# Two-layer decoder trunk: the high weight half of the SwiGLU products meets both row halves in one 512-column matmul, the two result halves added when the tile is read

## The chip, the core and the metric

The kernel runs on one core of a Trainium2 chip. The metric is the device time of one execution in microseconds (us). Times of three runs are known for the kernel before, and one further execution was recorded by the hardware profiler; its trace is what the rows below come from. In the rows, PE is TensorE's matmul, PEld TensorE's weight load, DVE VectorE, ACT ScalarE, POOL GpSimd and SP SyncE; L12 is line 12 of the kernel.

## What is computed

Two layers of a decoder trunk work on one sequence of 256 positions with a model width of 1024. Each layer has three sub-layers: a SwiGLU, a token mixer (in layer 0 a gated linear recurrence, in layer 1 differential attention), and a second SwiGLU. So there are six sub-layers, s = 0 to 5, and four of them (0, 2, 3, 5) are SwiGLUs. Cut to what matters here:

```
for l in range(2):
    mod = silu(c) @ ada_w[l] + ada_b[l]           # shift, scale, gate of each sub-layer
    pre(h, j) = rmsnorm(h, norm_g[l, j]) * (1 + scale_j) + shift_j
    x = x + 0.5 * (1 + gate_0) * swiglu(pre(x, 0), ffn_wi[l, 0], ffn_wo[l, 0])
    x = x +       (1 + gate_1) * mixer_l(pre(x, 1))
    x = x + 0.5 * (1 + gate_2) * swiglu(pre(x, 2), ffn_wi[l, 1], ffn_wo[l, 1])

swiglu(h, wi, wo):  gt, up = split(h @ wi);  return (silu(gt) * up) @ wo     # 1024 -> 2 x 2816 -> 1024
```

All data are 32-bit floats.

## The kernel before

**Layout.** The rows are held transposed: 128 partitions are 128 of the 1024 model dimensions, 8 chunks make the width, and the 256 positions lie along the free axis. Every product is built of matmuls with a 128x128 block of weights as the stationary operand and 256 positions as the moving one.

**Split products.** Weights and rows are each split in a high part (`whi`, `hh`, `ah`, `xh`), rounded to the type fp32r, and a low part, the remainder (`wlo`, `hl`, `al`, `xl`). `mm3` (lines 361 to 365) issues three matmuls for a block of weights and a chunk of rows, all into the same 256 columns of a PSUM tile: high weights with high rows (L363), high weights with low rows (L364), low weights with high rows (L365). Each has a weight load of its own.

**A SwiGLU sub-layer** (`ffn`) has an in stage and an out stage. The in stage takes 22 units of weights of 1024x256, as 11 pairs of a gate and an up unit; a unit gives two column tiles of 128, each of 8 chunks of `mm3`. The first two pairs are special (they start before the norm is known, `in_first`, `in_second`, or, in sub-layer 0, come from the start of the kernel). The other nine pairs go through `in_rest` (L418) and `in_one` (L397): 36 tiles, 288 `mm3`. ScalarE then takes the SiLU of the gate tile straight from PSUM (L359 `gs<-mm`), VectorE multiplies it with the up tile from PSUM (L541 `us<-mm,gs`), and `split` writes `ah` (ScalarE, L491) and `al` (VectorE, L492). The out stage (`out_product`) multiplies these 22 chunks with `wo`: four pairs of tiles of 22 `mm3` each, 176 in all, with `residual` (L483) reading the PSUM tile to update `xT`. After each residual `scaled_chunk` makes the next sub-layer's `xh`, `xl` and sum of squares `ss`; `finish_norm` (L341) then multiplies `ss` with ones on TensorE. It stands in TensorE's order behind 14 `mm3` of the next sub-layer.

**The stream of weights.** One list of items, weight units and pieces of the modulation matrix `ada_w`, 1 MB each (768 KB for some), is loaded in order by SP's DMA queue into three buffers (`raws`, `bufs=3`). ScalarE and VectorE prepare each weight unit, in two halves each: L239 `whi<-raw` on ScalarE and L240 `wlo<-raw,whi` on VectorE, into three buffers (`whl`). An `ada_w` piece takes two dot products on VectorE (L193). `ensure` keeps the preparation two items ahead of use and the loads four; a load can start only when an earlier item's buffer has been read to the end by VectorE. Pieces of `ada_w` are spread over the in stages: most in sub-layers 0 and 3, fewer in 2, few in 5.

**PSUM.** Matmul tiles (`mm`) rotate through five banks of 512 columns; 256 or 258 of the columns are used. The functions that the change does not touch (mixers, `in_first`, `in_second`, `in_values`, `mixer_out`) go on using `mm3`.

Of the kernel before, what the change touches and what calls it, by code (L numbers as in the profile page):

```python
# [18 lines left out]
P = 128  # L19
S = 256  # L20
# [81 lines left out]
# columns of the packed vectors  # L102
# [11 lines left out]
def trunk(ctx: ExitStack, tc, xT_in, c_in, vecs, positions, lam_in, kc_in, ada_w, ffn_wi, ffn_wo,  # L114
# [18 lines left out]
    # ---------------------------------------------------------------- constants and inputs  # L133
# [34 lines left out]
    hh = const.tile([P, KD, S], F32R, name="hh")  # L168
    hl = const.tile([P, KD, S], F32R, name="hl")
# [3 lines left out]
    # ---------------------------------------------------------------- adaLN modulation  # L173
# [3 lines left out]
    class Ada:  # L177
        """Part of one of the vectors (w: 0 shift, 1 scale, 2 gate) of sub-layer s: n chunks of 128 from chunk d0."""
# [22 lines left out]
    def finish(s, w, ds):  # L201
        """Adds the bias and makes what the sub-layer needs of the vector's chunks ds."""
        def vecs_of(name):
            if (name, s) not in mod_a:
                mod_a[name, s] = small.tile([P, KD], F32, name=name, tag=name, bufs=2)
            return mod_a[name, s]
        m = vecs_of(f"mod{w}")
        sm = sums[s, w]
        bias = vec[:, V_AB + (s * 3 + w) * KD:V_AB + (s * 3 + w + 1) * KD]
        V.tensor_tensor(out=m[:, ds], in0=sm[:, ds], in1=bias[:, ds], op=ALU.add)  # L210
        if w == 1:
            a = vecs_of("mod_a")
            V.scalar_tensor_tensor(out=a[:, ds], in0=m[:, ds], scalar=1.0,
                                   in1=vec[:, V_NG + s * KD:V_NG + (s + 1) * KD][:, ds], op0=ALU.add, op1=ALU.mult)
        elif w == 2:
            g = vecs_of("mod_g")
            V.tensor_scalar(out=g[:, ds], in0=m[:, ds], scalar1=1.0, scalar2=1.0 if s % 3 == 1 else 0.5,
                            op0=ALU.add, op1=ALU.mult)

    # ---------------------------------------------------------------- the stream of weights  # L220
# [21 lines left out]
    def ensure(i):  # L242
        """Make the i-th item ready; keep loads and splits running ahead of it."""
        for lim, done, what in ((LD, done_dma, "dma"), (LP, done_prep, "prep")):
            while done[0] <= min(i + lim, len(items) - 1):
                j = done[0]
                done[0] += 1
                if what == "prep":
                    while done_dma[0] <= j:
                        items[done_dma[0]].dma()  # L250
                        done_dma[0] += 1
                getattr(items[j], what)()
# [5 lines left out]
    def plan():  # L258
        gate = [Ada(0, 2, k, 2) for k in range(0, KD, 2)]
        for s in range(NSUB):  # L260
# [28 lines left out]
            # spread the coming modulation over this sub-layer's weights  # L289
# [21 lines left out]
    # ---------------------------------------------------------------- shared pieces  # L311
    def scaled_chunk(s, d, squares=True):
        """x * norm_g * (1 + scale), split in two parts of 12 bits, and the sum of squares."""
        a = mod_a["mod_a", s][:, d:d + 1]
        A.activation(out=xh[:, d, :S], in_=xT[:, d], func=AF.Copy, scale=a)
        V.scalar_tensor_tensor(out=xl[:, d, :S], in0=xT[:, d], scalar=a, in1=xh[:, d, :S].bitcast(F32),
                               op0=ALU.mult, op1=ALU.subtract)
        if squares:
            square_chunk(d)
# [26 lines left out]
    def table(name):  # L346
        """Change the set of functions on ScalarE, after everything that uses the set before."""
        with ExitStack() as es:
            for u in users:
                es.enter_context(tc.issue_after(u))  # L350
            ins = A.preload_act_table_set(name)  # L351
        tc.keep_in_program_order(ins)
        users.clear()
        tab[:] = [ins.ins]

    def fact(**kw):
        """A function of the present set."""
# [8 lines left out]

    def in_tile(w, c0, lo=0, hi=KD, acc=None):
        """One column tile from the rows before their norm, with the shift's product as one more column."""
# [5 lines left out]
    def in_first(s, keys):  # L374
        """The first column tiles of a sub-layer start before its norm is known: the last chunk comes at the end."""
# [10 lines left out]
    def scaled(acc):  # L386
        """The norm's factor on a tile of in_first; the shift's part is left to a bias."""
        c = small.tile([P, 1], F32, name="col", tag="col", bufs=8)
        V.tensor_copy(out=c, in_=acc[:, S:S + 1])
        t = tmp.tile([P, S], F32, name="post", tag="post", bufs=4)  # L390
# [14 lines left out]
    def in_values(w, v):  # L405
        """256 columns with the positions on the partitions."""
# [11 lines left out]
    def in_rest(s, keys):  # L418
        return [in_one(w, c) for w in (get(k) for k in keys) for c in range(2)]

    def drive(filler, active):
        """Emits one product tile, then the next stage of everything under way."""
# [16 lines left out]
    def mixer_out(s, yh, yl, late):  # L439
        """The output product of a mixer; the first tiles begin with the heads before the last pair."""  # L440
# [53 lines left out]
    def out_product(s, ws_of, K, yh, yl):  # L494
        """Both 128-column tiles of each pair; ws_of(d) lists the pair's units."""
        for dp in range(4):
# [3 lines left out]
            for w in ws:  # L500
                for c in range(2):
                    for k in range(w.K):
                        mm3(acc[c][:, :S], w, k, c * P, yh[k0 + k], yl[k0 + k], k0 + k == 0, k0 + k == K - 1)
# [3 lines left out]
            for c in range(2):  # L507
                residual(s, dp * 2 + c, acc[c])

    # ---------------------------------------------------------------- SwiGLU  # L510
    def ffn(s, first=None):
        with tc.tile_pool(name=f"ffn{s}", bufs=1, reuse_waits="tile") as fp:
            ah, al = [], []
            for f2 in range(KF // 2):
# [19 lines left out]
                for c in range(2):  # L534
# [9 lines left out]
                    h_ = fp.tile([P, S], F32R, name=f"ah{f}")  # L544
                    l_ = fp.tile([P, S], F32R, name=f"al{f}")
                    split(h_, l_, us)
                    ah.append(h_)
                    al.append(l_)
            table("natural_log_exp_and_others")
            out_product(s, lambda dp: [get((s, "wo", dp, i)) for i in range(len(WO_K))], KF, ah, al)  # L550

    # ---------------------------------------------------------------- HGRN2
    def hgrn2(s):
        with tc.tile_pool(name="hg", bufs=2, reuse_waits="tile") as hp, \
# [3 lines left out]
            # softmax over the single layer's axis, cumulated, less its first row  # L558
# [15 lines left out]
            def decay(p, f, lf, k_):  # L574
                """log f and 1 - f of two heads from the clamped f projections."""
# [43 lines left out]
            def core(h, q, k_, lf, v, g):  # L619
# [8 lines left out]
                # decays between the positions of each level and its middle  # L628
                E = hp.tile([P, 8, 2, P], F32, name="E")
                for t in range(2):  # L630
# [6 lines left out]
                    # levels 32 and 64, then the half of level 128 that this tile needs  # L637
# [22 lines left out]
                # att[s, t], level by level  # L660
# [46 lines left out]
    # ---------------------------------------------------------------- differential attention  # L707
    def rope_tables():
# [10 lines left out]
        # the nearest multiple of 2 pi, taken away in parts whose products are exact  # L719
# [24 lines left out]
    def diff_attention(s):  # L744
        with tc.tile_pool(name="at", bufs=2, reuse_waits="tile") as hp, \
                tc.tile_pool(name="aty", bufs=1, reuse_waits="tile") as yp:
            cs, sn = rope
            # lambda on every partition
# [119 lines left out]
    # ---------------------------------------------------------------- the trunk  # L868
    def start():
        """The first sub-layer's modulation comes in parts, each followed by its share of the first products."""  # L870
# [116 lines left out]
```

## Time and profile before

| | us |
|---|---|
| three runs: median (lowest to highest) | 1096.46 (1096.31 to 1098.94) |
| span of the profiled execution | 1094.7 |
| PE busy | 1079.3 |
| DVE busy | 835.2 |
| ACT busy | 600.4 |

The span goes from the first to the last instruction. The mean granted clock of TensorE over it is 0.998 of full speed. Busy times are sums over the span and say little by themselves; a wait is put down to what ended it. A matmul's recorded duration includes the pipeline behind it, so neighbours overlap: the step from one start to the next is what a matmul costs TensorE in a dense stream.

### The profile page before, as it was taken

Reading aid. Unit: us, or ns where it says so; the run is one execution under the profiler, and the core shown is the slowest. Engines: PE = TensorE matmul, PEld = TensorE weight load, DVE = VectorE, ACT = ScalarE, POOL = GpSimd, SP = SyncE. Lnnn points to the kernel's source line nnn. Section 1 sums busy time; section 2 is a strip of 40 time slices with the busy share of each in tenths; the row PEclk is TensorE's granted clock in tenths of the full one; section 3 lists DMA queues with packets and bytes.
Section 4 is the critical chain, followed back from the end, with each engine's and each line's share of the span. In section 5 each row is a group of like instructions: output and inputs, shape, how many; then the busy total and the mean of one; then the engine's idle time right before and its main releaser. Section 6 shows DMA issues by size and latency. Waiting matters only on the chain.

```text
span 1094.7 us, 21064 instructions
## 1 busy us (share of the span) xinstructions
PE 1079.3 (99%) x8662; PEld 1056.1 (96%) x8662; DVE 835.2 (76%) x1577; ACT 600.4 (55%) x1038; POOL 2.6 (0%) x12
## 2 busy tenths in 40 slices
PE   6999999999999999999999999999999999999998
PEld 3899999999999899999999999999999999999998
DVE  5888888599876699786658888955999979765542
ACT  4444644486775575545447444544778876444431
POOL 0000000000000000000000000000000000000000
PEclk9999999999999999999999999999999999999999
DMA  9878889556643158886554888965357625766460
GB/s 370 311 278 317 298 319 320 209 211 247 231 176 116 40 192 304 328 297 253 214 190 154 337 316 342 322 231 201 137 213 254 234 109 193 271 230 229 154 214 20
DMA packets 38306, 256.67 MB, mean 234 GB/s; under 512 B 4161, under 2 KB 6593, under 8 KB 9154
## 3 DMA queue, kind: packets, MB, share of 16 engines
q1 hardware_dynamic: 38210, 255.32, 63.8%
q8 instruction: 68, 1.11, 0.4%
q14 instruction: 28, 0.23, 0.1%
HBM read 254.26 MB, written 1.05 MB: 233 GB/s over the span
## 4 chain that ended last, share of the span: by engine, by line
PE 92%; DVE 3%; ACT 3%; DMA 2%; issue 1%; DVEq 0%
PE mm L363 26%; PE mm L364 26%; PE mm L365 26%; PE aux L670 1%; PE mm L413 1%; PE mm L412 1%; DMA rawa<-in_ada_w_dram 1%; PE mm L414 1%; DVE rawa L193 1%; PE mm L903 1%; PE aux L903 1%; ACT L351 1%; ACT whi L239 1%; PE aux L796 1%; PE aux L825 1%
## 5 line engine op out<-in xcount | busy, mean ns | idle before, releaser
L240 DVE TENSOR_TENSOR wlo<-raw,whi 128x1024 fp32r<-128x1024 f32 (+1 forms) x336 | 393.3, 1195 | 148.6 <-ACT whi L239 147.8
L239 ACT ACTIVATE whi<-raw 128x1024 fp32r<-128x1024 f32 (+1 forms) x336 | 335.7, 1032 | 236.8 <-PE mm L364 95.4
L363 PE MATMUL mm<-hh,whi 128*128 128x256 f32 x1376 | 391.9, 285 | 0.0
L364 PE MATMUL mm<-hl,whi 128*128 128x256 f32 x1376 | 390.3, 284 | 0.0
L365 PE MATMUL mm<-hh,wlo 128*128 128x256 f32 x1376 | 389.3, 283 | 0.0
L363 PEld LDWEIGHTS mm<-hh,whi 128*128 128x128 f32 x1376 | 263.9, 192 | 0.6
L364 PEld LDWEIGHTS mm<-hl,whi 128*128 128x128 f32 x1376 | 263.9, 192 | 0.4
L365 PEld LDWEIGHTS mm<-hh,wlo 128*128 128x128 f32 x1376 | 263.9, 192 | 0.2
L363 PE MATMUL mm<-ah,whi 128*128 128x256 f32 x704 | 199.2, 283 | 0.0
L364 PE MATMUL mm<-al,whi 128*128 128x256 f32 x704 | 199.2, 283 | 0.0
L365 PE MATMUL mm<-ah,wlo 128*128 128x256 f32 x704 | 199.2, 283 | 0.0
L193 DVE CUSTOM_DVE_ANT_0 rawa<-rawa,cact 128x1024 f32<-128x1024 f32 x144 | 172.7, 1219 | 20.8 <-DMA rawa<-in_ada_w_dram 14.8
L363 PEld LDWEIGHTS mm<-ah,whi 128*128 128x128 f32 x704 | 135.2, 192 | 0.0
L364 PEld LDWEIGHTS mm<-al,whi 128*128 128x128 f32 x704 | 135.2, 192 | 0.0
L365 PEld LDWEIGHTS mm<-ah,wlo 128*128 128x128 f32 x704 | 135.2, 192 | 0.0
L363 PE MATMUL mm<-xh,whi 128*128 128x258 f32 x288 | 81.8, 287 | 0.0
L364 PE MATMUL mm<-xl,whi 128*128 128x258 f32 x288 | 81.4, 284 | 0.0
L365 PE MATMUL mm<-xh,wlo 128*128 128x258 f32 x288 | 81.1, 283 | 0.0
L491 ACT ACTIVATE ah<-us 128x256 fp32r<-128x256 f32 x88 | 35.4, 411 | 76.8 <-DVE us L541 73.6
L364 PEld LDWEIGHTS mm<-xl,whi 128*128 128x128 f32 x288 | 54.5, 190 | 0.2
L365 PEld LDWEIGHTS mm<-xh,wlo 128*128 128x128 f32 x288 | 54.4, 190 | 0.1
L363 PEld LDWEIGHTS mm<-xh,whi 128*128 128x128 f32 x288 | 54.0, 189 | 0.2
(207 smaller groups left out, 1289.7 us busy)
## 6 DMA issues: line engine op xcount, KB each, us to landing
raw<-in_ffn_wi_dram SPq DMA_DIRECT2D x88, 1024.0 KB, 5.2
rawa<-in_ada_w_dram SPq DMA_DIRECT2D x71, 1024.0 KB, 5.2
raw<-in_ffn_wo_dram SPq DMA_DIRECT2D x32, 1024.0 KB, 5.0
raw<-in_a_w_in_dram SPq DMA_DIRECT2D x16, 1024.0 KB, 4.9
raw<-in_ffn_wo_dram SPq DMA_DIRECT2D x16, 768.0 KB, 4.3
raw<-in_b_w_in_dram SPq DMA_DIRECT2D x12, 1024.0 KB, 4.9
raw<-in_a_w_out_dram SPq DMA_DIRECT2D x4, 1024.0 KB, 4.9
raw<-in_b_w_out_dram SPq DMA_DIRECT2D x4, 1024.0 KB, 4.9
```

Source lines behind the costliest of these rows:

```text
L193: V.tensor_tensor_reduce(out=self.raw[:, d], in0=self.raw[:, d], in1=cact, scale=1.0, scalar=0.0, op0=ALU.mult, op1=ALU.add, accum_out=sum ...
L239: A.activation(out=self.hi[:, sl], in_=self.raw[:, sl], func=AF.Copy)
L240: V.tensor_tensor(out=self.lo[:, sl], in0=self.raw[:, sl], in1=self.hi[:, sl].bitcast(F32), op=ALU.subtract)
L351: ins = A.preload_act_table_set(name)
L363: PE.matmul(acc, wh, rh, start=start, stop=False)
L364: PE.matmul(acc, wh, rl, start=False, stop=False)
L365: PE.matmul(acc, wl, rh, start=False, stop=stop)
L412: PE.matmul(acc[:, :2 * P], xh_, wh, start=k == 0, stop=False)
L413: PE.matmul(acc[:, :2 * P], xl_, wh, start=False, stop=False)
L414: PE.matmul(acc[:, :2 * P], xh_, wl, start=False, stop=k == KD - 1)
L491: A.activation(out=hi, in_=src, func=AF.Copy)
L903: PE.matmul(t[:, :S + 2], w.raw[:, k, c0:c0 + P], xs[:, k], start=k == 0, stop=k == KD - 1)
```

## The change

For the nine later pairs of each SwiGLU's in stage and for the whole out stage, `mm3` is replaced by `mm2`. High and low rows now lie side by side in one tile (`hx`, `a2`: two times 256 columns), and the high weights meet both in one matmul of 512 columns; the low weights meet the high rows in a second matmul of 256 columns, which adds to the first 256 columns of the tile. When a tile is read, `joined` copies columns 256 to 511 out of PSUM on ScalarE and adds the first 256 columns to the copy on VectorE. Everything that read the PSUM tile before reads this sum in SBUF instead. On the last chunk the two matmuls swap places. The tag `post` gets six buffers in place of four. Comments are dropped without effect.

```diff
-    hh = const.tile([P, KD, S], F32R, name="hh")
-    hl = const.tile([P, KD, S], F32R, name="hl")
+    hx = const.tile([P, KD, 2, S], F32R, name="hx")
+    hh, hl = hx[:, :, 0], hx[:, :, 1]
...
+    def mm2(acc, w, k, c0, x2, start, stop):
+        wh, wl = w.hi[:, k, c0:c0 + P], w.lo[:, k, c0:c0 + P]
+        both = x2.rearrange("p a s -> p (a s)")
+        if not stop:
+            PE.matmul(acc, wh, both, start=start, stop=False)
+        PE.matmul(acc[:, :S], wl, x2[:, 0], start=False, stop=False)
+        if stop:
+            PE.matmul(acc, wh, both, start=start, stop=True)
+
+    def joined(acc):
+        t = tmp.tile([P, S], F32, name="post", tag="post", bufs=6)
+        A.activation(out=t, in_=acc[:, S:], func=AF.Copy)
+        V.tensor_tensor(out=t, in0=acc[:, :S], in1=t, op=ALU.add)
+        return t
+
+    def in_two(w, c):
+        acc = mm_tile()
+        for k in range(KD):
+            mm2(acc, w, k, c * P, hx[:, k], k == 0, k == KD - 1)
+        return joined(acc), None
...
     def in_rest(s, keys):
-        return [in_one(w, c) for w in (get(k) for k in keys) for c in range(2)]
+        return [in_two(w, c) for w in (get(k) for k in keys) for c in range(2)]
...
-    def out_product(s, ws_of, K, yh, yl):
+    def out_product(s, ws_of, K, y2):
...
-                        mm3(acc[c][:, :S], w, k, c * P, yh[k0 + k], yl[k0 + k], k0 + k == 0, k0 + k == K - 1)
+                        mm2(acc[c], w, k, c * P, y2[k0 + k], k0 + k == 0, k0 + k == K - 1)
...
-                residual(s, dp * 2 + c, acc[c])
+                residual(s, dp * 2 + c, joined(acc[c]))
...
-                    h_ = fp.tile([P, S], F32R, name=f"ah{f}")
-                    l_ = fp.tile([P, S], F32R, name=f"al{f}")
-                    split(h_, l_, us)
-                    ah.append(h_)
-                    al.append(l_)
+                    a2.append(fp.tile([P, 2, S], F32R, name=f"a{f}"))
+                    split(a2[-1][:, 0], a2[-1][:, 1], us)
```

## Rows read from the trace of the kernel before

**Rows 1.** The profile's page: busy time, and the chain that ended last
```profile
PE 1079.3 (99%) x8662; PEld 1056.1 (96%) x8662; DVE 835.2 (76%) x1577; ACT 600.4 (55%) x1038; POOL 2.6 (0%) x12
PE 92%; DVE 3%; ACT 3%; DMA 2%; issue 1%; DVEq 0%
```

**Rows 2.** Busy time by stage: in stages of sub-layers 0, 2, 3, 5; out stage of 0
```profile
core 0: us, PE busy (x) PEld busy (x) DVE busy (x) ACT busy (x) POOL busy (x), PEclk, DMA share, GB/s
51.00:154.90 103.90, 103.90 (x867) 103.87 (x866) 90.00 (x148) 53.61 (x82) 0.00 (x0) 1.00 0.80 293
154.90:218.20 63.30, 63.30 (x530) 63.30 (x529) 45.17 (x69) 28.38 (x39) 0.10 (x1) 1.00 0.76 271
412.30:516.00 103.70, 103.70 (x867) 103.70 (x866) 84.97 (x129) 50.13 (x75) 0.00 (x0) 1.00 0.80 298
602.90:706.50 103.60, 103.60 (x865) 103.60 (x865) 90.55 (x142) 49.09 (x73) 0.00 (x0) 1.00 0.88 329
924.20:1027.90 103.70, 103.70 (x867) 103.70 (x866) 68.11 (x98) 48.73 (x73) 0.00 (x0) 1.00 0.63 226
```

**Rows 3.** Groups by line: in stage of sub-layer 2 (288), out stages together (704)
```profile
L364 PE MATMUL mm<-hl,whi 128*128 128x256 f32 x288 | 81.5, 283 | 0.0
...
L363 PE MATMUL mm<-ah,whi 128*128 128x256 f32 x704 | 199.2, 283 | 0.0
```

**Rows 4.** Timeline of PE (start us, duration us): two 512-column matmuls among 256-column ones
```profile
297.60 0.28 PE L363 MATMUL mm<-hh,whi 128*128 128x256 f32 x1
297.71 0.28 PE L364 MATMUL mm<-hl,whi 128*128 128x256 f32 x1
297.83 0.39 PE L635 MATMUL aux<-mseg,lh 128*128 128x512 f32 x1
298.06 0.40 PE L636 MATMUL aux<-mseg,ll 128*128 128x512 f32 x1
298.29 0.28 PE L365 MATMUL mm<-hh,wlo 128*128 128x256 f32 x1
298.41 0.28 PE L363 MATMUL mm<-hh,whi 128*128 128x256 f32 x1
```

**Rows 5.** Timeline of PE: ten fp32 matmul records of the start, merged
```profile
36.41 2.34 PE L903 MATMUL mm<-xs,raw 128*128 128x258 f32 x10
```

**Rows 6.** Groups by line: nearest rows to the copy and the add
```profile
L359 ACT ACTIVATE gs<-mm 128x256 f32<-128x256 f32 x72 | 26.9, 376 | 37.6 <-PE mm L365 37.4
...
L391 DVE TENSOR_TENSOR post<-mm,rstd 128x256 f32<-128x256 f32 x41 | 16.7, 415 | 0.0
```

**Rows 7.** Timeline of DVE: a 256-column operation with another right behind it
```profile
109.34 0.43 DVE L492 TENSOR_TENSOR al<-us,ah 128x256 fp32r<-128x256 f32 x1
109.68 1.22 DVE L240 TENSOR_TENSOR wlo<-raw,whi 128x1024 fp32r<-128x1024 f32 x1
```

**Rows 8.** Waits (us in total, times, longest), in stages of sub-layers 0, 3 and 2
```profile
ACT whi L239 <- DMA raw<-in_ffn_wi_dram: 23.3, 9, 3.3
...
ACT whi L239 <- DMA raw<-in_ffn_wi_dram: 13.7, 11, 4.0
...
ACT whi L239 <- PE mm L364: 15.7, 9, 2.4
```

**Rows 9.** Timeline of DVE: the last in unit's low half, sub-layers 0 and 3
```profile
142.19 2.36 DVE L240 TENSOR_TENSOR wlo<-raw,whi 128x1024 fp32r<-128x1024 f32 x2 [1.61 <-ACT whi L239]
...
694.25 1.23 DVE L240 TENSOR_TENSOR wlo<-raw,whi 128x1024 fp32r<-128x1024 f32 x1
```

**Rows 10.** Timeline at the turn from sub-layer 2 to 3: DVE, then PE
```profile
580.33 0.48 DVE L483 SCALAR_TENSOR_TENSOR xT<-mm,mod_g,xT 128x256 f32<-128x256 f32 x1
580.85 2.36 DVE L240 TENSOR_TENSOR wlo<-raw,whi 128x1024 fp32r<-128x1024 f32 x2
583.53 0.42 DVE L327 TENSOR_TENSOR ss<-ss,sq 128x256 f32<-128x256 f32 x1
...
584.40 0.59 PE L341 MATMUL aux<-ss,ones 128*128 128x256 f32 x2
```

**Rows 11.** Timeline of the last instructions
```profile
1091.11 0.28 PE L365 MATMUL mm<-ah,wlo 128*128 128x256 f32 x1
1091.43 0.48 DVE L483 SCALAR_TENSOR_TENSOR xT<-mm,mod_g,xT 128x256 f32<-128x256 f32 x1 [1.67 <-PE mm L365]
```

More of the change, by code (lines that the diff above doesn't have):

```diff
@@ L389, in scaled @@
         V.tensor_copy(out=c, in_=acc[:, S:S + 1])
-        t = tmp.tile([P, S], F32, name="post", tag="post", bufs=4)
+        t = tmp.tile([P, S], F32, name="post", tag="post", bufs=6)
         V.tensor_tensor(out=t, in0=acc[:, :S], in1=rstd, op=ALU.mult)
@@ L507, in out_product @@
             for c in range(2):
-                residual(s, dp * 2 + c, acc[c])
+                residual(s, dp * 2 + c, joined(acc[c]))
     def ffn(s, first=None):
         with tc.tile_pool(name=f"ffn{s}", bufs=1, reuse_waits="tile") as fp:
-            ah, al = [], []
+            a2 = []
             for f2 in range(KF // 2):
@@ L543, in ffn @@
                         V.scalar_tensor_tensor(out=us, in0=up, scalar=col, in1=gs, op0=ALU.add, op1=ALU.mult)
-                    h_ = fp.tile([P, S], F32R, name=f"ah{f}")
-                    l_ = fp.tile([P, S], F32R, name=f"al{f}")
-                    split(h_, l_, us)
-                    ah.append(h_)
-                    al.append(l_)
+                    a2.append(fp.tile([P, 2, S], F32R, name=f"a{f}"))
+                    split(a2[-1][:, 0], a2[-1][:, 1], us)
             table("natural_log_exp_and_others")
-            out_product(s, lambda dp: [get((s, "wo", dp, i)) for i in range(len(WO_K))], KF, ah, al)
+            out_product(s, lambda dp: [get((s, "wo", dp, i)) for i in range(len(WO_K))], KF, a2)
     def hgrn2(s):
```

## The prediction

> **What bounds the kernel now.** I read four views, in this order. First the page: TensorE is busy for 1079.3 of 1094.7 us and makes 92% of the chain that ended last [rows 1], so time is saved only where a TensorE step gets shorter, and lost where TensorE has to wait. Second, busy time by stage: in the four in stages TensorE has no gap, at full granted clock (1.00), while VectorE is busy for 90.0, 85.0, 90.6 and 68.1 of some 103.7 us [rows 2]. VectorE is thus the next limit, and in sub-layers 0 and 3 it is close. Third, the steps: busy time of matmuls overlaps, so the cost is the step between starts. An in stage has 3 x 288 matmuls of 256 columns [rows 3], and 864 x 0.12 = 103.7 us is its whole length [rows 2]: the step is 120 ns, always. Fourth, the waits of the stream of weights, which say whether it is TensorE that holds the supply back or the supply that is late [rows 8].
>
> **TensorE: what one chunk saves.** Now a chunk costs 3 x 120 = 360 ns. After the change it is one matmul of 512 columns and one of 256. No SwiGLU matmul has 512 columns today, but the gated recurrence has some, of the same types: L635 starts at 297.83, L636 at 298.06, the next matmul of 256 columns at 298.29, the one after it 0.12 later [rows 4]. That is 0.46 us for two steps; seven other pairs without idle time beside them show 0.46 or 0.47. So a 512-column step is 230 to 235 ns, and I take 232. The columns are the same 768 before and after; what goes is the part of a step that doesn't grow with the columns: 2 x 120 - 232 = 8 ns per chunk. Chunks: 4 x 288 = 1152 in the in stages and 704 in the out stages [rows 3], together 1856. 1856 x 8 ns = **14.8 us saved**. Bounds: at 235 ns 5 ns (9.3 us); at 230 ns, and with the 256-column step behind a 512-column one 5 ns under 120 (the 0.12 is read to 0.01), 15 ns (27.8 us).
>
> A rule speaks against even this. The Trainium skill, "TensorE: Matmul & The Clock Gate", section "Back-to-back issue gap", gives a warm step of columns/2.4 GHz + 2.5 ns, so 109 ns for 256 columns and 216 for 512: a chunk would save 2.5 ns, by estimate 4.7 us in all. The trace disagrees at both sizes (120 and 232), so rows carry the sum.
>
> **The added reads.** Each finished tile now needs a copy of half of it on ScalarE and an add on VectorE: 36 tiles in each in stage, 8 in each out stage, 176 in all. Nearest rows: ScalarE reading 256 columns from PSUM 376 ns, VectorE with one operand from PSUM 415 ns [rows 6]. Where another VectorE instruction stands ready behind, one of this size takes 0.34 us from start to start [rows 7]. So an in stage gets 36 x 0.38 = 13.7 us on ScalarE, which has 50 of 104 us busy and covers it, and 36 x 0.34 to 0.42 = 12.2 to 15.1 us on VectorE. SiLU and product go on as before, only from SBUF, at nothing: they are neither removed nor added. PSUM tiles stay five, each filled for 2.8 us, so a read that is late by less than some 10 us holds no bank back. The new wait is the add's, for the copy: behind it on VectorE stand the low halves of the next unit's weights, and for these TensorE waits. Off the path in sub-layers 2 and 5, on it in 0 and 3:
>
> The new in stage is 288 x 0.352 = 101.4 us on TensorE. *Sub-layer 0:* VectorE needs 90.0 + 12.2 to 15.1 = 102.2 to 105.1 us. It may end late by its present lead: the last unit is ready at 142.19 + 2.36 = 144.6 [rows 9] and is used at 51.0 + 17 x 48 x 0.12 = 148.9, so 4.4 us. Of 101.4 + 4.4 us it may then idle for 0.7 to 3.6, middle 2.1; now it idles for 13.9. *Sub-layer 3:* 102.8 to 105.7 us of work, a lead of 602.9 + 97.9 - 695.5 = 5.3 us, idle allowed 1.0 to 3.9, middle 2.4; now 13.1. This idle time is mostly VectorE waiting, through ScalarE, for a load to land (23.3 and 13.7 us of ScalarE's waits [rows 8]), and a load can only start when VectorE has read an older buffer to the end. An add that runs while a load is under way costs nothing; one that runs with the data already there delays the next load. I take it that two thirds of the idle time get filled, because the loads run on while VectorE adds: 4.6 and 4.4 us are left, so TensorE waits 2.5 + 2.0 = **4.5 us lost**. Bounds: all of it filled, 0; none, 11.8 + 10.7 = 22.5 us. *Sub-layer 2:* 97.2 to 100.1 us of work in 101.4, and the supply there waits for TensorE (15.7 us [rows 8]): nothing. *Sub-layer 5:* 68.1 + 15.1: nothing. The out stages have room (45.2 of 63.3 us [rows 2]).
>
> **The turns between sub-layers.** Behind sub-layers 0, 2 and 3 the last tile's residual leads to the sum of squares, which ends at 583.53 + 0.42 = 583.95; TensorE takes it at 584.40 [rows 10], 0.45 us later. Copy and add put 0.38 + 0.42 and some 0.1 for the hand-overs, 0.9 us, ahead of it: 0.45 us of wait, if the order of VectorE and ScalarE holds. In between stands a unit's preparation (2.36 us [rows 10]); if the copy or add slips behind it, the wait is up to 2.8; if the preparation moves back, 0. I take 0.7, nearest to the order that the rows show: 3 x 0.7 = **2.1 us lost** (0 to 8.4). The mixers' ends are untouched.
>
> **The tail.** Now the residual starts 0.04 us after the last matmul's end (1091.39, 1091.43 [rows 11]). Copy and add stand in between, with nothing to hide them: **0.9 us lost**.
>
> **Sum.** -14.8 + 4.5 + 2.1 + 0.9 = -7.3 us. The profiled span of 1094.7 us becomes 1087.4. The median of the runs is 1.8 us above that span, and I carry the change over to it: 1096.46 - 7.3 = **1089.2 us**.
>
> **Rivals.** *1. VectorE and the ring of three load buffers become the bound.* Place: in stages of sub-layers 0 and 3; price: 22.5 us, the adds filling no idle time; it decides as soon as more than about 2 us of VectorE's idle time per stage remain and outweighs the gain when over 8 us remain. For it: VectorE at 87% there, the supply already late (ScalarE waits for loads). Against: that idle time is waiting for transfers, which don't need VectorE. Time 1096.5 - 14.8 + 3.0 + 22.5 = 1107; with half the idle time filled 1094.
>
> *2. The 120 ns are set by the weight load, and a 512-column matmul hides it whole.* Then the 512-column step is that of a stream that is surely wider than its load: ten records at the start take 2.34 us [rows 5], less the last one's 0.39 (as in [rows 4]) over nine steps, 217 ns. A chunk would cost 337, saving 23 ns, 42.7 us; in stages 0 and 3 TensorE would need 97.1 us and the supply would take back 2 x 4.3. 1089.2 - 27.8 + 8.6 = 1070. Against: all eight pairs stand at 230 to 235. The Trainium skill, same page, section "LDWEIGHTS (loading the stationary operand)", gives a 128-column load as 107 ns by its rule of columns/1.2 GHz; that is under 120 and would fit either reading.
>
> *3. A step is columns alone, and the change doesn't do what it says.* 512 columns would take 2 x 120 = 240. Nothing is saved; with TensorE at 103.7 us the supply costs hardly anything. 1096.5 + 3.0 = 1099.5. For it: 256 columns at the granted 2.4 GHz are 107 ns and the step is 120, so part of a step's excess may well grow with them. Against: the eight pairs again. It is the skill's rule above (nearly all columns, almost nothing fixed) put to this kernel's own step.
>
> **How the numbers follow.** Forecast case 62%, rival 1 18%, rival 2 8%, rival 3 10%, anything else 2%. A measurement of this kernel tells about 0.3% from no change: under 1093.2 is faster, over 1099.7 slower. The forecast case with all bounds of its terms spreads from 1072 (27.8 us saved, 3.0 lost) to 1096; a tenth of it is not faster. Faster: 0.56 + 0.08 + 0.03 of rival 1. Same: 0.06 + 0.04 of rival 1 + 0.06 of rival 3. Slower: 0.11 of rival 1 + 0.04 + 0.02. The range of 1072 to 1103 leaves out half of rival 2 and the upper half of rival 1.
>
> **What would show it.** In the trace after: steps of 232 and 120 ns in turn in the SwiGLU stages (217 is rival 2, 240 rival 3); an out stage of 176 x 0.352 = 62.0 us instead of 63.4; in stages of sub-layers 2 and 5 at 101.4 us. In stages of sub-layers 0 and 3 longer than that by 2 to 3 us, with TensorE waiting for VectorE's low weights, and VectorE busy for over 95% of them; over 104 us is rival 1. A gap of under 1 us ahead of L341's successor, and 0.9 us more between last matmul and last store. The prediction is wrong if the order in which copies and adds are queued makes VectorE wait for TensorE, for then even the quiet stages lose.

## The result and the profile after

The changed kernel takes 1083.78 us (median of four runs, 1083.49 to 1088.16), the kernel before on the same chip 1096.38 (1096.26 to 1098.94): a ratio of 0.988, 95% interval 0.9866 to 0.9895, so 12.6 us less. The forecast was 7.3 us less, 1089.2. The execution that was profiled first was the one of 1088.16 us, with a wait that is shown further down; the rows of "after" are therefore from a second profile of the same kernel (`r_again` below; span 1082.3, its run 1084.12).

| | before | after |
|---|---|---|
| span of the profiled execution | 1094.7 | 1082.3 |
| start up to the first in stage | 51.02 | 52.54 |
| in stage of sub-layer 0 / 2 / 3 / 5 | 103.86 / 103.67 / 103.67 / 103.67 | 101.63 / 101.53 / 101.51 / 101.51 |
| out stage of sub-layer 0 / 2 / 3 / 5 | 63.36 / 63.36 / 63.36 / 63.36 | 62.00 / 61.44 / 61.66 / 61.66 |
| TensorE matmul records | 8662 | 6806 |
| VectorE busy, ScalarE busy | 835.2, 600.4 | 895.7, 658.5 |

A stage runs from the start of its first matmul to the start of the first matmul behind it (the last one to where such a matmul would start); the edges in [rows 2] are rounded to 0.1 us.

First the page of the kernel after, as in [rows 1]: busy time, the chain's shares by engine, and the two groups that the change adds (count, then busy us and mean ns of one, then idle time ahead of them and what ended it).

```profile
PE 1065.9 (98%) x6806; PEld 957.6 (88%) x6806; DVE 895.7 (83%) x1753; ACT 658.5 (61%) x1214; POOL 2.6 (0%) x12
PE 94%; ACT 2%; DMA 1%; DVE 1%; issue 0%; DVEq 0%
...
L380 ACT ACTIVATE post<-mm 128x256 f32<-128x256 f32 x176 | 67.1, 381 | 125.3 <-PE mm L375 124.2
L381 DVE TENSOR_TENSOR post<-mm,post 128x256 f32<-128x256 f32 x176 | 73.7, 421 | 33.1 <-ACT post L380 32.7
```

TensorE has 6806 matmuls, 1856 fewer, one for each chunk, and still makes 94% of the chain. The 176 copies take 381 ns and the 176 adds 421 ns, as the nearest rows had it (376, 415 [rows 6]). TensorE's weight loading, which had no idle time in the in stages [rows 2], now has some.

Then the stages of the kernel after, in the order of [rows 2] but with the out stage second (stretch, its length, busy time of each engine, granted clock, DMA share, GB/s):

```profile
52.54:154.17 101.63, 101.63 (x578) 88.44 (x577) 98.05 (x178) 64.06 (x115) 0.00 (x0) 1.00 0.78 287
154.17:216.18 62.01, 62.01 (x354) 53.85 (x353) 50.73 (x80) 32.45 (x49) 0.14 (x1) 1.00 0.80 295
410.04:511.57 101.53, 101.53 (x578) 88.27 (x577) 96.23 (x164) 61.32 (x110) 0.00 (x0) 1.00 0.81 305
596.72:698.23 101.51, 101.51 (x578) 88.31 (x577) 98.46 (x174) 59.24 (x106) 0.00 (x0) 1.00 0.86 319
914.87:1016.38 101.51, 101.51 (x579) 88.27 (x577) 81.50 (x133) 60.11 (x108) 0.00 (x0) 1.00 0.64 230
```

All four in stages have nearly the same length, 101.51 to 101.63 us, and TensorE is busy for the whole of each. 101.51 / 288 = 352.4 ns per chunk, against 360. In the out stages a chunk is a little cheaper still: 61.66 / 176 = 350.3 ns. The two in which VectorE is busy for 96 to 97% (sub-layers 0 and 3) take no more than 0.12 us longer than the one in which it is busy for 80%: inside the in stages the supply of weights costs nothing.

By spans the 12.4 us lie as follows: in stages -8.7 (2.23 + 2.14 + 2.16 + 2.16); out stages -6.7 (1.36 + 1.92 + 1.70 + 1.70); from the end of an out stage to the next in stage -0.2 (sub-layer 1), +0.2 (turn to 3) and +0.7 (sub-layer 4); tail +0.8; start +1.5. The start is loading and modulation, which the change doesn't touch. In the profiles of the changed kernel and its variants it ends at 51.6 to 53.3, in the one profile of before at 51.02; whether that is chance stays open.

### The profile page after: what moved, and what is told of

Read it like the earlier page. It is cut to its first block, busy times and chain, and to the rows that moved or that the text cites. A ratio compares the mean times of both kernels' runs of the same rounds, so it can differ in the third digit from the quotient of the medians.

```text
span 1086.4 us, 17708 instructions
## 1 busy us (share of the span) xinstructions
PE 1066.2 (98%) x6806; PEld 957.7 (88%) x6806; DVE 895.6 (82%) x1753; ACT 657.7 (61%) x1214; POOL 2.6 (0%) x12
## 4 chain that ended last, share of the span: by engine, by line
PE 87%; DMA 4%; DVE 4%; ACT 3%; issue 1%; DVEq 0%; ACTq 0%; SPq 0%
PE mm L372 33%; PE mm L373 18%; PE mm L363 6%; PE mm L364 6%; PE mm L365 6%; PE mm L375 4%; DMA rawa<-in_ada_w_dram 3%; PE mm L923 1%; DVE rawa L193 1%; DVE wlo L240 1%; PE aux L690 1%; PE mm L436 1%; PE mm L435 1%; PE mm L437 1%; DMA raw<-in_ffn_wo_dram 1%; ACT whi L239 1%
## 5 line engine op out<-in xcount | busy, mean ns | idle before, releaser
L372 PE MATMUL mm<-hx,whi 128*128 128x512 f32 x1008 | 361.7, 398 | 0.0
L373 PE MATMUL mm<-hx,wlo 128*128 128x256 f32 x1152 | 299.9, 281 | 0.0
L372 PE MATMUL mm<-a,whi 128*128 128x512 f32 x672 | 238.1, 397 | 0.9 <-ACT whi L239 0.9
L373 PEld LDWEIGHTS mm<-hx,wlo 128*128 128x128 f32 x1152 | 217.5, 189 | 13.4
L372 PEld LDWEIGHTS mm<-hx,whi 128*128 128x128 f32 x1008 | 189.7, 188 | 39.3
L373 PE MATMUL mm<-a,wlo 128*128 128x256 f32 x704 | 192.8, 281 | 0.8 <-DVE wlo L240 0.8
L372 PEld LDWEIGHTS mm<-a,whi 128*128 128x128 f32 x672 | 126.6, 189 | 29.3 <-ACT whi L239 1.2
L373 PEld LDWEIGHTS mm<-a,wlo 128*128 128x128 f32 x704 | 133.6, 190 | 4.5 <-DVE wlo L240 1.6
L381 DVE TENSOR_TENSOR post<-mm,post 128x256 f32<-128x256 f32 x176 | 73.4, 419 | 35.1 <-ACT post L380 34.8
L363 PE MATMUL mm<-hx,whi 128*128 128x256 f32 x224 | 65.9, 294 | 0.0
L364 PE MATMUL mm<-hx,whi 128*128 128x256 f32 x224 | 64.2, 286 | 0.0
L365 PE MATMUL mm<-hx,wlo 128*128 128x256 f32 x224 | 63.5, 283 | 0.0
L375 PE MATMUL mm<-hx,whi 128*128 128x512 f32 x144 | 57.3, 398 | 0.0
```

The costliest lines, as they stand in the source:

```text
L363: PE.matmul(acc, wh, rh, start=start, stop=False)
L364: PE.matmul(acc, wh, rl, start=False, stop=False)
L365: PE.matmul(acc, wl, rh, start=False, stop=stop)
L372: PE.matmul(acc, wh, both, start=start, stop=False)
L373: PE.matmul(acc[:, :S], wl, x2[:, 0], start=False, stop=False)
L375: PE.matmul(acc, wh, both, start=start, stop=True)
```

## The experiments

**The same kernel once more** (`r_again`), to see what a second profile shows.

> The changed kernel once more, unaltered, for a second profile: the first profiled execution took 1088.2 us with TensorE waiting 2.2 us around 191 us, the other three 1083.5 to 1084.0. If that wait is a rare event: 1083.6 us, no wait in the out stage of sub-layer 0, span near 1081.8. If it belongs to the kernel (the adds use up the supply's lead in sub-layer 0): the wait is there again.

1084.55 us (1082.99 to 1085.74) against 1097.93 for the kernel before on that chip: ratio 0.9877 (0.9858 to 0.9896), the same result. What differs from the first profile is a wait in sub-layer 0's out stage. There, TensorE in the first profile:

```profile
191.38 0.28 PE L373 MATMUL mm<-a,wlo 128*128 128x256 f32 x1
192.60 0.50 PE L372 MATMUL mm<-a,whi 128*128 128x512 f32 x1 [0.93 <-ACT whi L239]
...
193.85 0.38 PE L373 MATMUL mm<-a,wlo 128*128 128x256 f32 x1 [0.76 <-DVE wlo L240]
```

The weights came late, and this stage took 65.48 us there against 62.00 in the second profile. TensorE waited 0.93 + 0.76 = 1.7 us of that; behind the waits its granted clock was 0.50, the lower of its two levels (1.2 GHz), from 194.9 to 198.3 us, which makes most of the rest. ScalarE, which makes the high half, was itself waiting for a load (`[1.60 <-DMA raw<-in_ffn_wo_dram]` at 191.49). The second profile shows no wait of TensorE there, but no reserve either. For the same unit, the second low half, then the first matmul that uses it:

```profile
191.26 1.22 DVE L240 TENSOR_TENSOR wlo<-raw,whi 128x1024 fp32r<-128x1024 f32 x1
...
192.64 0.28 PE L373 MATMUL mm<-a,wlo 128*128 128x256 f32 x1
```

It is ready at 192.48 and used at 192.64. In the kernel before, the same half was ready 5.2 us ahead of its use (188.82, 194.00). So the adds of sub-layer 0's in stage use up the lead that the out stage behind it lives on, and a late load is seen by TensorE.

**Without the added reads** (`e_nojoin`): the matmuls of the changed kernel, the tiles read without copy and add.

```
     def joined(acc):
-        t = tmp.tile([P, S], F32, name="post", tag="post", bufs=6)
-        A.activation(out=t, in_=acc[:, S:], func=AF.Copy)
-        V.tensor_tensor(out=t, in0=acc[:, :S], in1=t, op=ALU.add)
-        return t
+        return acc[:, :S]
```

> Copy and add are left out: readers take the first half of the tile alone, so the high weights' product with the low rows is missing from the result. TensorE's work is that of the changed kernel. Theory (the adds fill VectorE's idle time and cost only latency, 0.9 us at the tail and some tenths at three turns): 1082.2 us, 1.4 us under the changed kernel. Rival (the supply of sub-layers 0 and 3 pays for the adds, as the prediction had it, 4.5 us more): 1077 to 1079 us.

1081.26 us, ratio 0.9848 (0.9828 to 0.9869), so all 176 copies and adds cost some 3.2 us by the ratios, with intervals that overlap. The total lies between what the theory and the rival said and decides nothing. The stages do. In stages of sub-layers 0 and 3 without the reads:

```profile
51.72:153.35 101.63, 101.63 (x579) 88.44 (x577) 88.89 (x146) 53.93 (x82) 0.00 (x0) 1.00 0.80 299
...
595.47:696.98 101.51, 101.51 (x578) 88.25 (x577) 88.38 (x140) 49.30 (x73) 0.00 (x0) 1.00 0.86 328
```

101.63 and 101.51, to the hundredth what they are with the reads, while VectorE is busy for 9 to 10 us less. What the reads cost lies elsewhere: by spans 2.7 us, of which 0.8 is the start, 0.8 the tail, 0.35 sub-layer 0's out stage (62.00 against 61.66), and 0.7 the stretch from sub-layer 3's out stage to sub-layer 5's in stage (154.98 against 154.31), where only the turn ahead has added reads. The turn into sub-layer 3 is 0.2 longer, the out stage ahead of it 0.2 shorter.

**The same reads, the old steps** (`e_split256`): the 512-column matmul in two of 256, so three matmuls per chunk again, and the join kept.

```
-            PE.matmul(acc, wh, both, start=start, stop=False)
+            for a in range(2):
+                PE.matmul(acc[:, a * S:(a + 1) * S], wh, both[:, a * S:(a + 1) * S],
+                          start=start and a == 0, stop=stop and a == 1)
```

> The 512-column matmul is issued as two of 256 columns with the same weights, each half into its own columns; copy and add stay. Theory (the gain is the step's fixed part, 360 - 352 ns per chunk, and nothing else): steps of 120 ns again, 1083.6 + 1856 x 0.0076 = 1097.7 us, 1.4 us above the kernel before. Rival (much of the gain is from something else, as from PSUM tiles freed earlier): clearly under 1095 us.

1099.80 us (1098.53 to 1101.19), ratio 1.0015 (1.0003 to 1.0028). In stages of sub-layers 0 and 3:

```profile
51.85:155.71 103.86, 103.86 (x867) 103.83 (x866) 99.38 (x179) 64.56 (x116) 0.00 (x0) 1.00 0.78 290
...
604.11:707.79 103.68, 103.68 (x867) 103.68 (x866) 98.99 (x173) 59.18 (x107) 0.00 (x0) 1.00 0.86 324
```

867 matmuls and 103.68 to 103.86 us, as before [rows 2], with the weight load busy throughout, as the theory had it; nothing else makes the gain. The wider matmul alone is thus worth 15.3 us (1099.80 - 1084.55), and the join costs 1.65 us (0.3 to 3.1 by the interval) where TensorE's step is 120 ns.

**128 columns at a time** (`e_128`): the same columns in four and two matmuls, to see whether a step has a part that doesn't shrink.

```
+        def piece(w_, n):
+            for a in range(n):
+                PE.matmul(acc[:, a * P:(a + 1) * P], w_, both[:, a * P:(a + 1) * P], ...)
...
-        PE.matmul(acc[:, :S], wl, x2[:, 0], start=False, stop=False)
+        piece(wl, 2)
```

> Every matmul of the changed chunk is cut to 128 columns: four for the high weights, two for the low. Theory (a step is a fixed part of some 8 ns and 0.436 ns per column): 63 to 65 ns each, 378 to 390 ns per chunk instead of 352, 1131 to 1153 us. Rival (a weight load of some 107 to 120 ns paces every matmul, and 512 columns hide it): 6 x 107 to 120 = 640 to 720 ns per chunk, 1620 to 1770 us.

1678.2 us in a single run. The in stage of sub-layer 0, then the group of one line (count, busy us, mean ns of one):

```profile
51.97:245.07 193.10, 193.10 (x1730) 193.07 (x1729) 110.04 (x190) 62.77 (x116) 0.00 (x0) 1.00 0.50 173
...
L373 PE MATMUL mm<-hx,whi 128*128 128x128 f32 x4608 | 679.6, 275 | 0.0
```

An in stage has 6 x 288 = 1728 matmuls and takes 193.10 us: 111.7 ns each, at the full granted clock (1.00). The theory (a fixed part and 0.436 ns per column) said 63 to 65 and is refuted, the rival's 107 to 120 fits; with weights of its own a matmul of half the columns saves only 8 ns, and the engine's weight loading is busy all the while. The Trainium skill, "TensorE: Matmul & The Clock Gate", section "LDWEIGHTS (loading the stationary operand)", gives a 128-column load as 107 ns; the 111.7 agree with that to 5 ns. The Trainium skill, same page, section "Back-to-back issue gap", gives a sustained 81 ns for a matmul of 128 columns, and the trace disagrees.

**Uneven columns** (`e_sizes`): the 512 as 384 + 128, the 256 as 192 + 64.

```
-        PE.matmul(acc[:, :S], wl, x2[:, 0], start=False, stop=False)
+        piece(wl, (0, 192, 256), False)
...
-            PE.matmul(acc, wh, both, start=start, stop=False)
+            piece(wh, (0, 384, 512), False)
```

> The changed chunk is cut otherwise: high weights with 384 and 128 columns, low weights with 192 and 64, so that steps of four sizes stand in one stream. The cut to 128 columns gave steps of 112 ns throughout. Theory (a step is the longer of a weight-bound floor of 112 ns and a column part with 117 to 120 ns at 256 and 235 ns at 512 columns, so 0.45 ns per column): 192, 128 and 64 columns all at 112, 384 at 176, the chunk 512 ns, 1083.6 + 1856 x 0.160 = 1380 us. Rival (128 columns took 112 ns because narrow matmuls of this type run slower per column, not because of the weights): 64 columns clearly under 112 ns, 192 columns clearly over 112.

1683.26 us in a single run, at a mean granted clock of 0.805. Three stretches: one early, one whole in stage, and one out stage:

```profile
60.00:115.00 55.00, 55.00 (x434) 54.96 (x434) 33.55 (x62) 18.84 (x34) 0.00 (x0) 1.00 0.57 208
...
637.40:784.00 146.60, 146.60 (x1154) 146.53 (x1153) 95.41 (x158) 56.79 (x106) 0.00 (x0) 1.00 0.61 213
...
1116.60:1285.60 169.00, 169.00 (x707) 169.00 (x705) 38.58 (x55) 31.92 (x48) 0.00 (x0) 0.50 0.21 71
```

Where the clock is 1.00 a chunk takes 146.60 / 288 = 509 ns, close to the sum that the theory named. Its single steps don't fit: the starts stand 258 (384 columns), 60 (128), 139 (192) and 51 ns (64) apart, where 176, 112, 112 and 112 were expected. Taken word for word, these steps show the rival's signs (64 columns under 112, 192 over). But a step of 60 ns for 128 columns contradicts the 112 of `e_128`, so single starts can't be trusted as prices here; the run decides between theory and rival for no one size. In the third stretch the granted clock was half (0.50), and a chunk took 169.00 / 176 = 960 ns. That is why the total misses the 1380 of the theory: the clock was at 0.50 for two stretches of 324.3 us each (121.0 to 445.3 and 964.1 to 1288.3). At 509 in place of 960 ns per chunk they would be 305 us shorter, by estimate 1378 us in all.

**A second VectorE operation per join** (`e_add2`), to see how much room VectorE has left.

```
         V.tensor_tensor(out=t, in0=acc[:, :S], in1=t, op=ALU.add)
+        V.tensor_tensor(out=t, in0=t, in1=t, op=ALU.max)
```

> After each add VectorE takes the maximum of the sum with itself: the same value, one more 256-column operation of 0.34 to 0.42 us per tile, 36 per in stage. Theory (in sub-layers 0 and 3 the changed kernel has used up the supply: 98.0 and 98.5 us of VectorE work in 101.5, the last unit ready 0.4 and 0.9 us ahead of its use): nothing is left to fill, 12 to 15 us more in each, 0 to 4 us in sub-layer 2, 1.7 us at turns and tail: 1106 to 1117 us. Rival (VectorE work beside the loads is free here, the adds would have cost nothing in any number): 1086 us.

1103.61 us (1102.06 to 1106.4), ratio 1.0048 (1.0031 to 1.0064). In stages of sub-layers 0, 2, 3 and 5, then who waits in sub-layer 3 (us in total, times, longest), one of these waits in the timeline with the two low halves that it waits for, and the stretch behind it:

```profile
52.06:164.10 112.04, 106.42 (x579) 90.56 (x578) 106.41 (x210) 62.32 (x114) 0.00 (x0) 0.97 0.68 253
423.91:526.00 102.09, 101.23 (x579) 87.85 (x577) 101.43 (x192) 58.82 (x107) 0.00 (x0) 1.00 0.77 288
611.39:718.30 106.91, 103.61 (x578) 89.08 (x577) 105.56 (x203) 57.48 (x105) 0.00 (x0) 0.98 0.80 299
936.69:1038.20 101.51, 101.51 (x578) 88.26 (x577) 93.14 (x167) 59.63 (x108) 0.00 (x0) 1.00 0.64 230
...
PE mm L373 <- DVE wlo L240: 3.3, 3, 1.8
...
686.92 2.36 DVE L240 TENSOR_TENSOR wlo<-raw,whi 128x1024 fp32r<-128x1024 f32 x2
...
688.19 0.39 PE L373 MATMUL mm<-hx,wlo 128*128 128x256 f32 x1 [1.76 <-DVE wlo L240]
...
688.61:692.03 3.42, 3.42 (x12) 2.87 (x12) 3.42 (x8) 0.81 (x2) 0.00 (x0) 0.50 0.96 395
```

The total is 19.1 us over the changed kernel (1084.55 in `r_again`; the kernel before has 1097.93 in both comparisons), where the theory had 22 to 33: right in kind, too dear by at least 3 us. The profiled execution is the slowest of the four (1106.4). In it sub-layer 0's stage grows by 10.4 us and sub-layer 3's by 5.4, sub-layer 2's by 0.6, sub-layer 5's not at all (the out stages behind 0 and 3 by 3.6 and 1.4), and TensorE waits for VectorE's low weights. That is the mechanism of the first rival, in its place.

Waiting is only part of the growth. TensorE is idle for 5.6 of the 10.4 us (112.04 - 106.42) and for 3.3 of the 5.4. Behind two of the waits in sub-layer 0 (94.7 and 122.0 us) and the one shown in sub-layer 3 the granted clock stood at 0.50 for 3.4 us each, and a chunk took 0.64 us instead of 0.352. By estimate from these numbers that is 1.5 us lost each time, 3 and 1.5 us. The rows also show that TensorE needs a unit's low weights by halves: it goes on at 688.19, when the first of the two is done, not at 689.28, when the second is.

**One half of the change alone** (`e_in_only`: the out products as before; `e_out_only`: the in products as before).

```
-                        mm2(acc[c], w, k, c * P, y2[k0 + k], ...)
+                        mm3(acc[c][:, :S], w, k, c * P, y2[k0 + k][:, 0], y2[k0 + k][:, 1], ...)
...
-                residual(s, dp * 2 + c, joined(acc[c]))
+                residual(s, dp * 2 + c, acc[c])
```

```
-        return [in_two(w, c) for w in (get(k) for k in keys) for c in range(2)]
+        return [in_one(w, c) for w in (get(k) for k in keys) for c in range(2)]
```

> Only the in stages take the 512-column matmul, copy and add; the out stages go back to three matmuls and read PSUM directly. Theory (the gain is the step, 7.6 ns on each of 1152 chunks; turns and tail as before the change): 8.8 us under the kernel before, 1087.6 where that takes 1096.4. Rival (the supply of sub-layers 0 and 3 takes back 4.5 us): 4 us under it, 1092.

> Only the out stages take the 512-column matmul, copy and add. Theory: 704 x 7.6 ns = 5.4 us saved, less 0.9 us at the tail and some 0.5 at the turns: 4.0 us under the kernel before, 1092.4 where that takes 1096.4. Rival (turns cost 0.7 us or more each, as the prediction had it): 2.4 us under it, 1094.

1089.04 us, ratio 0.992 (0.9905 to 0.9935), so -8.9 against 1097.93; and 1093.83 us, ratio 0.9967 (0.9955 to 0.9978), so -4.1. Sub-layer 0's in stage and the last out stage of the first, then of the second:

```profile
53.05:154.68 101.63, 101.63 (x578) 88.42 (x577) 98.02 (x178) 63.96 (x115) 0.00 (x0) 1.00 0.77 287
1021.88:1085.39 63.51, 63.51 (x529) 63.30 (x527) 25.68 (x30) 20.22 (x23) 0.00 (x0) 1.00 0.39 133
```

```profile
52.48:156.34 103.86, 103.86 (x867) 103.83 (x866) 90.65 (x149) 54.37 (x82) 0.00 (x0) 1.00 0.80 293
1025.42:1087.47 62.05, 62.05 (x354) 53.79 (x352) 28.15 (x36) 22.43 (x29) 0.00 (x0) 1.00 0.40 132
```

Each half shortens its own stages and leaves the other's alone, and -8.9 - 4.1 = -13.0 lies between the -12.6 and -13.4 of both together: within the intervals the halves add up. One out stage is an exception: in `e_in_only` sub-layer 0's takes 64.16 us where the three others take 63.4, with a wait of 0.6 us for low weights. `e_out_only`, without adds in the in stages, has no such wait.

**The residual in two VectorE steps** (`e_res2`): both halves of an out tile go straight into the residual, with no copy and no add.

```
+        for a in range(2 if s % 3 != 1 else 1):
+            V.scalar_tensor_tensor(out=xT[:, d], in0=acc[:, a * S:(a + 1) * S], scalar=..., in1=xT[:, d], ...)
...
-                residual(s, dp * 2 + c, joined(acc[c]))
+                residual(s, dp * 2 + c, acc[c])
```

> The out stages' copy and add are replaced: the residual takes the two halves of the PSUM tile in two steps on VectorE, 0.48 us each, so the way from the last matmul to the residual's end has 0.96 us instead of 0.38 + 0.42 + 0.48 and hand-overs. Theory (turns and tail are latency): 0.4 us less at the tail, 0 to 0.4 at each of three turns, 0.4 to 1.2 us under the changed kernel. Rival (copy and add are hidden at the turns, the tail is all): 0.4 us.

1084.18 us, ratio 0.9877 (0.9862 to 0.9891): no different from the changed kernel. The end of the trace shows the part that did change:

```profile
1078.36 0.40 PE L375 MATMUL mm<-a,whi 128*128 128x512 f32 x1
...
1078.80 1.00 DVE L507 SCALAR_TENSOR_TENSOR xT<-mm,mod_g,xT 128x256 f32<-128x256 f32 x2 [1.11 <-PE mm L375]
```

From the last matmul's start to the end of the residual 1.44 us, against 1.80 with copy and add (rows below): 0.36 us less, too little to be told in the total, so theory and rival stay undecided.

**Further in the same direction** (`e_best`): `e_res2`, and the mixers' column tiles on two matmuls per chunk as well.

```
     def in_one(w, c, second=False):
...
-        acc = mm_tile()
-        for k in range(KD):
-            mm3(acc[:, :S], w, k, c * P, hh[:, k], hl[:, k], k == 0, k == KD - 1)
-        return acc[:, :S], None
+        return in_two(w, c)
```

> The residuals in two VectorE steps, as in e_res2, and also the 28 later in tiles of both mixers (224 chunks) on the 512-column matmul with copy and add. Theory (7.6 ns per chunk also there): 1.7 us under the changed kernel, less the adds' latency in two stages that aren't bound by TensorE throughout: 0.5 to 1.5 us under it. Rival (VectorE is the limit in the mixers, 28 adds of 0.34 to 0.42 us go on the path): 5 to 10 us over it.

1085.33 us (1082.95 to 1086.22), ratio 0.9875 (0.9857 to 0.9893): not faster than the changed kernel. The two mixers' in stages:

```profile
234.35:348.41 114.06, 113.27 (x795) 101.06 (x794) 100.12 (x237) 82.93 (x162) 1.87 (x6) 1.00 0.56 201
...
780.88:857.17 76.29, 76.28 (x502) 69.66 (x501) 74.06 (x202) 64.45 (x175) 0.00 (x0) 1.00 0.59 210
```

They are shorter by 1.1 and 3.2 us (115.13 and 79.49 in the changed kernel), but from the second of them to sub-layer 5's in stage it took 57.8 us for 54.2, and that in stage 103.5 for 101.5. In the first of these TensorE waits 1.8 us for ScalarE (squares and transposed tiles of attention) where it waited for nothing before, in the second 1.8 us once for low weights (at 924.45). Neither theory nor rival had this; of a gain in the total nothing is left.

## Why the prediction was right, and where it was not

**The step: right in its sum.** The prediction put a chunk at 232 + 120 = 352 ns, and in the in stages it is 352.4. In the timeline of the kernel after, in sub-layer 0's in stage:

```profile
100.59 0.40 PE L372 MATMUL mm<-hx,whi 128*128 128x512 f32 x1
100.83 0.28 PE L373 MATMUL mm<-hx,wlo 128*128 128x256 f32 x1
100.94 0.39 PE L372 MATMUL mm<-hx,whi 128*128 128x512 f32 x1
101.17 0.28 PE L373 MATMUL mm<-hx,wlo 128*128 128x256 f32 x1
101.29 0.40 PE L372 MATMUL mm<-hx,whi 128*128 128x512 f32 x1
```

0.24, 0.11, 0.23, 0.12: over sub-layer 5's in stage the steps average 235 ns after a 512-column matmul and 117 ns after a 256-column one. Both parts were 3 ns off, in opposite directions; that the sum fits so well is partly luck. In the in stages 7.5 ns per chunk went, in the out stages 9.7, 15.4 us together by the stages' lengths (14.8 forecast), and `e_split256` gives 15.3 back when the wide matmul is cut in two again. Rival 2 (a chunk of 337 ns) and rival 3 (360) both fall. The reason that the prediction gave, a part of each step that doesn't grow with the columns, is supported only for 256 columns and more. Below that something else sets the step: `e_128` stands at 112 ns where a fixed part and columns would give about 64. What the fixed part is made of, and why a chunk is 2 ns cheaper in the out stages, no run here settles.

**The supply: the term that was too big.** The prediction had TensorE wait 2.5 + 2.0 us in the in stages of sub-layers 0 and 3; it waits for nothing there. What the supply does cost lies in the out stage of sub-layer 0: 0.3 us in the second profile (62.00 for 61.66), 3.8 in the first. Its picture was right in kind: the adds run while loads are under way, the lead shrinks, and ScalarE waits less for loads (23.3 and 13.7 us [rows 8]). The two rows of the kernel after that answer to these, sub-layer 0 then 3, then the second low half of the last unit in each stage, as in [rows 9], and the matmul that first uses it in sub-layer 0:

```profile
ACT whi L239 <- DMA raw<-in_ffn_wi_dram: 1.8, 4, 0.6
...
ACT whi L239 <- DMA raw<-in_ffn_wi_dram: 4.3, 7, 1.9
...
146.84 1.22 DVE L240 TENSOR_TENSOR wlo<-raw,whi 128x1024 fp32r<-128x1024 f32 x1
...
690.48 1.22 DVE L240 TENSOR_TENSOR wlo<-raw,whi 128x1024 fp32r<-128x1024 f32 x1
...
150.17 0.28 PE L373 MATMUL mm<-hx,wlo 128*128 128x256 f32 x1
```

**The lead.** The last unit's second half is ready at 146.84 + 1.22 = 148.06 and used at 150.17, in the fifth of the tile's eight chunks; in sub-layer 3 ready at 691.70, used at 694.23. So 2.1 and 2.5 us of lead are left. The prediction set the time at which the second half is ready against the unit's first matmul, 1.7 to 1.9 us too early: in the kernel before, the leads were not 4.4 and 5.3 us but 6.2 (144.55, used at 150.80) and 7.0 (695.48, used at 702.44). With that alone mended, its own sum gives 0.7 + 0.3 us of waiting instead of 2.5 + 2.0. **This is the largest error of the prediction: the lead, in the supply's term.**

**Idle time and the add.** Two smaller sizes were off in the same direction. VectorE's idle time is 101.63 - 98.05 = 3.6 and 101.51 - 98.46 = 3.0 us, a quarter of the 13.9 and 13.1 before; the prediction left a third (4.6 and 4.4). And the add is cheap: work and idle time over the new stage and the 4.1 us of lead that were used up come to 105.7 us in sub-layer 0, less 3.6 idle and the old 90.0 is 12.1 for 36 adds, 0.34 us each; for sub-layer 3 it is 0.34 too. The prediction took the middle of 0.34 to 0.42. By this estimate the two are worth some 2.6 us per stage.

The last unit is not the one with the least to spare: the eighth unit of sub-layer 3 has its first half ready at 635.78 and uses it at 636.43, 0.65 us later. So the kernel is close to the edge, as `e_add2` shows.

**The turns: smaller than forecast.** 0.7 us each were charged for three. The turn from sub-layer 2 to 3, as in [rows 10]: first the row of VectorE in the kernel before that comes just ahead of those, then VectorE and TensorE after.

```profile
579.59 0.49 DVE L316 SCALAR_TENSOR_TENSOR xl<-xT,mod_a,xh 128x256 fp32r<-128x256 f32 x1 [0.58 <-ACT xh L315]
...
573.62 0.42 DVE L381 TENSOR_TENSOR post<-mm,post 128x256 f32<-128x256 f32 x1 [0.37 <-ACT post L380]
...
575.28 2.36 DVE L240 TENSOR_TENSOR wlo<-raw,whi 128x1024 fp32r<-128x1024 f32 x2
577.95 0.42 DVE L327 TENSOR_TENSOR ss<-ss,sq 128x256 f32<-128x256 f32 x1
...
578.15 0.28 PE L364 MATMUL mm<-xl,whi 128*128 128x258 f32 x1
578.42 0.70 PE L341 MATMUL aux<-ss,ones 128*128 128x256 f32 x2
```

The order held: 2.36 us of preparation stand ahead of the sum of squares in both kernels. Before, VectorE waited 0.58 us for the `xh` of the tile before the last; now the last tile's add runs in that gap. From the last matmul's end to the end of the sum of squares it was 583.95 - 579.52 = 4.43 us and is 578.37 - 573.17 = 5.20: 0.77 more, not 0.9. Then L341 follows its predecessor by 0.27 us instead of 0.12: 0.15 lost, and 0.1 more at the next matmul. The turn into sub-layer 4 shows the same, the one into sub-layer 1 nothing. Together some 0.5 us instead of 2.1. The 0.45 that the rows gave was thus high already, and what was added to it for a changed order did not come.

**The tail: right.** The end of the kernel after, as in [rows 11]:

```profile
1077.80 0.40 PE L375 MATMUL mm<-a,whi 128*128 128x512 f32 x1
1078.24 0.38 ACT L380 ACTIVATE post<-mm 128x256 f32<-128x256 f32 x1 [1.73 <-PE mm L375]
1078.66 0.42 DVE L381 TENSOR_TENSOR post<-mm,post 128x256 f32<-128x256 f32 x1 [1.16 <-ACT post L380]
1079.12 0.48 DVE L506 SCALAR_TENSOR_TENSOR xT<-post,mod_g,xT 128x256 f32<-128x256 f32 x1
```

From the last matmul's end (1078.20) to the residual's end (1079.60) 1.40 us, against 0.52 before: 0.9 more, as forecast.

**The sum.** By these terms -15.4 + 0 + 0.5 + 0.9 = -14.0 us. The profiled spans without their start differ by 13.9. The start's +1.5, on which the change has no hold, brings that to -12.4; the runs measure -12.6, and -13.4 in `r_again`. The sign and the largest term came from rows of the kernel before. Forecast and result are 5.3 us apart because the supply (4.5) and the turns (1.6) were charged too high and the gain of the steps (0.6) too low, less the start's 1.5. **Rival 1** didn't happen, but one more VectorE operation per tile brings it on.

## What to carry to other kernels

Where two matmuls share their weights, widening one of them saves little (here 7.5 to 9.7 ns of 360), so count the chunks first, and price the work that the join moves to other engines against the idle time of the stage in which it lands. Idle time that is waiting for transfers can be filled with short work (three quarters of it here). How much is left, the smallest lead of any unit tells, in that stage and in the one behind it; count it to the matmul that first needs the weights, not to the start of the unit. And read the length of a step as a mean over a whole stage: in `e_sizes` single starts gave no usable price.

## What was not expected of the hardware

Halving the columns of a matmul with weights of its own hardly makes it cheaper: `e_128` shows 111.7 ns for 128 columns at the full granted clock, against 120 for 256 columns before. Whether fewer columns still cost 112 was not settled (`e_sizes`). And in `e_sizes` the granted clock stood at 0.50, the lower of its two levels (1.2 GHz), over a whole out stage (1116.60 to 1285.60 us) with TensorE busy throughout, and a chunk took 960 ns instead of 509; it had run without a gap at 1.00 early on (60 to 115 us). The trace shows what stood ahead of both falls: a wait of TensorE, 1.0 us each time, for VectorE's low weights (at 121.0 us behind one more of 1.7), the first of them here:

```profile
120.34 0.41 PE L373 MATMUL mm<-hx,wlo 128*128 128x192 f32 x2 [1.03 <-DVE wlo L240]
```

The clock then stayed at 0.50 through all that was left of these narrow matmuls, without a gap, and was back at 1.00 some 3 us after they gave way to matmuls of 258 columns (442 and 1286 us). In sub-layers 2 and 5, where TensorE never waited in the SwiGLU stages, the same matmuls ran at 1.00 throughout. In `e_add2`, with 512 and 256 columns, the clock fell behind waits of 1.6 to 1.8 us too, but was back after 3.4 us. `e_128`, whose matmuls were narrow as well, kept a mean of 0.997; TensorE never waited in its SwiGLU stages. That the narrow matmuls are what kept the clock down is a reading of these rows; no run tried it.
